# Gated DeltaNet in a two-layer trunk: decay, A and attention matrices built transposed, right-hand side and solution scaled differently

## The chip, the cores and the metric

The kernel runs on one core of one Trainium2 chip. The metric is the time of one execution in device microseconds (us), as the median of several runs. The engines are called PE (matrix products), DVE (vector), ACT (scalar, activations), POOL (GpSimd) and SP (which here only issues DMAs).

## The reference

The kernel computes a two-layer decoder trunk on 256 tokens of 1024 features, all in float32. Layer 0 mixes tokens by retention, layer 1 by gated DeltaNet; a SwiGLU channel mixer follows each. Only DeltaNet is touched. Its core, for 16 value heads of 128 features (two value heads share one of 8 key heads), is

```
gcum = cumsum(g)                                   # g: log decay of a token
decay[i, j] = exp(gcum[i] - gcum[j])   for i >= j, else 0
A    = beta * (k k^T) * decay          for i > j,  else 0
[u, w] = (I + A)^-1 [beta v, beta k exp(gcum)]
attn = (q k^T) * decay                 for i >= j, else 0
v_new = u - w S;   o = q exp(gcum) S + attn v_new
S = S exp(g_last) + (k exp(g_last - gcum))^T v_new
```

k and q are L2-normalised; a short causal convolution and a SiLU come before. The output is normalised per head, gated by silu(z) and projected. The reference uses chunks of 64 tokens; the kernel uses two chunks of 128, which is the same function.

## The kernel before

**Main stream.** The trunk is one list of jobs. A job has one slab of weights (512 KB): SP loads it (L130), ACT rounds it to a high part `whi` (L131), DVE forms the rest `wlo` (L133), and PE forms three products of it with the split activations (L139 to L141). Three buffers of each kind exist, so a slab cannot be loaded before an older one has been used. DeltaNet's jobs come in the order z0, k, q, z1, v0, z2, v1, v2, v3, z3, and then the output projection. For the k, q and v jobs, the convolution's taps are one ACT and three DVE instructions for each 128 channels (`taps`, L721 and L724).

**Tasks.** All that is particular to DeltaNet runs in generators that are advanced one step after each job. A planner then puts the instructions of each engine in an order, from program order and its own estimates; on the chip each engine works its list in that order, and waits on semaphores.

**The tasks the change touches**, in order of time:
- `gates`: log decays, beta, and the matrix `D` of decays of each chunk and head, as exp of a product with a triangular mask (`decay`, L714 and L715). `D` has the row token i on the partitions.
- `amat`, after each pair of key heads: `A` = k k^T scaled by `beta2` and `D` (L768 to L778); small scale vectors at L754 to L762.
- `invert`: the matrix `V` = ((I + A)^-1)^T. The 32 x 32 diagonal blocks of all heads and chunks are brought through DRAM to one block per partition (`Ab`, L797, L799). 31 steps of forward substitution follow on DVE, two instructions each: an outer product `pr` (L813) and a subtraction from `Vb` (L815). Step i works on n = i + 1 by m = 31 - i elements. `Vb` goes through DRAM once more (`Vd`, `Vc`, L820, L823), is copied into `Vf` and transposed into `Tc` (L832, L833); then the blocks are merged to 64 and 128 by products (L848 to L882).
- `attn`: q k^T (L913), copied by ACT (L915), multiplied by `D` on POOL into `att` (L916), and then in `flush` transposed by PE (four L200 for one instruction of POOL) and copied back by ACT into the place of `D` (L904). There are eight such rounds.
- `v_T`: transposes v and scales it, one ACT instruction for each head and chunk (L1098).
- `inner`, for each group of four heads: `solve` (products with `V`, L937, and a copy `uu` by ACT, L939), `du` (L959), products with keys, queries and the state (L951), `attend` (L945), the combination (L976), norm and gate.

The substitution is spread over the jobs by an estimate of its cost:

```
            V.tensor_tensor(tmp, Vb[:, 0:n, i:i + 1].broadcast_to([P, n, m]),
                            Ab[:, n:32, i].unsqueeze(1).broadcast_to([P, n, m]), ALU.mult)
            V.tensor_tensor(Vb[:, 0:n, n:32], Vb[:, 0:n, n:32], tmp, ALU.subtract)
            cost += 0.4 + 2 * n * m / 960
            if cost > b["pace"]:
```

Of the kernel before, what the change touches and what calls it, by code (L numbers as in the profile page):

```python
# [10 lines left out]
F32 = mybir.dt.float32  # L11
# [6 lines left out]
P = 128  # L18
D = 1024
# [11 lines left out]
def shape_constants():  # L31
    """Constants that depend on the shapes alone: identity, triangular masks,
    retention decay (with the key scale) and the rotary frequencies."""
# [14 lines left out]
def turn_pieces():  # L48
    """1 / (2 pi) cut into 12-bit pieces."""
# [12 lines left out]
class Trunk:  # L62
    """The main stream is a list of jobs, one weight slab each; tasks (generators)
    are advanced one step after every job, so that their small products and
    elementwise work lie between the large products."""
# [13 lines left out]
    # ------------------------------------------------------------ jobs and tasks  # L79
# [27 lines left out]
    def prefetch(self, ahead):  # L107
        """Loads slabs in the order of the jobs until ahead of them wait behind the next."""
        while self.todo and len(self.slabs) <= ahead:
            n = self.todo.pop(0)  # L110
            self.slabs[n] = self.slab(*self.jobs[n][1])

    # ---------------------------------------------------------------- helpers
# [9 lines left out]
    def slab(self, w, k0, nk, c0, ncol):  # L123
        """Rows [k0*128, (k0+nk)*128), columns [c0, c0+ncol) of w as the exact
        pair hi + lo of 12-bit parts."""
# [17 lines left out]
    def proj_tok(self, w, c0, ncol, xT, nk, done, parts=None, pair=(), tile_done=None):  # L143
        """[tokens, columns] products: one PSUM tile for each token tile, given to done.
        parts: ranges of the rows, other jobs may come between them (a list of lists of
        jobs is returned then). pair: numbers of slabs whose work on the second token
        tile waits for the next slab."""
# [3 lines left out]
        for n, k0 in enumerate(ks):  # L151

            def fn(hi, lo, n=n, k0=k0):
# [4 lines left out]
                for t, work in ((0, first), (1, held)):  # L158
# [3 lines left out]
                    # the second token tile not before the first where that one is wanted early  # L162
# [18 lines left out]
    def proj_chan(self, w, c0, xT, done):  # L181
        """[columns, tokens] products for 256 columns: one PSUM tile [128, 2, 256].
        A job is one block of 128 columns."""
# [18 lines left out]
    # ------------------------------------------------------------------ setup  # L202
# [63 lines left out]
    def load_gain(self, row):  # L266
        """A gain on all partitions."""
# [3 lines left out]
    # ------------------------------------------------------------------- norm  # L271
# [3 lines left out]
    def sumsq(self, half):  # L275
        """Adds up h^2 / D over a half of the features, for each token."""
# [5 lines left out]
    def rstd(self):  # L282
        """r[token tile] = (mean h^2 + eps)^-1/2 as [128, NT]."""
# [11 lines left out]
    def load_T(self, src, gain, half):  # L295
        """Half of the features of two [128, 1024] token tiles -> transposed, times
        the gain of each feature, as hi/lo pair in xh, xl [128, 8, 256]."""
# [15 lines left out]
    def rstd1(self, t):  # L313
        """(mean h^2 + eps)^-1/2 of one token tile, eps being in its first sum."""
# [12 lines left out]
    def out_proj(self, w, yT, nk, nxt, early=None):  # L327
        """h += y w, and what the next sublayer (kind, layer) needs of h. early: slabs of
        the first half done before those of the second half begin."""
# [56 lines left out]
    # -------------------------------------------------------------------- FFN  # L386
# [48 lines left out]
    # -------------------------------------------------------------- retention  # L435
    def rope_tables(self, b):
        """cos and sin of the rotary angles times r of the token: [128, 256]."""
# [159 lines left out]
    # ------------------------------------------------------------------ gated DeltaNet  # L597
# [12 lines left out]
    def normed(self, out, t, half, r):  # L610
        """Half of the features of h r gain, for one token tile."""
# [6 lines left out]
    def gdn_tokens(self, t, r):  # L618
        """Normalised, transposed tokens."""
# [13 lines left out]
    def gates(self, b):  # L633
# [52 lines left out]
        for c in range(NT):  # L686
            for hg in range(4):
# [5 lines left out]
                if len(pend) == 3:  # L693
                    self.decay(b, Ur, *pend.pop(0))
# [499 lines left out]
```

## Time and profile before

| | us |
|---|---|
| median of 3 runs | 874.71 |
| the three runs | 877.99, 874.71, 874.05 |
| span of the profiled execution, first to last instruction | 876.3 |

The profiled execution has no time of its own beside its span. DeltaNet's own work lies between about 420 and 660 us of the span. A profile gives for each engine how long it was busy, and for idle time the instruction that ended it; matmuls are pipelined, so that PE counts as busy from the start of one to the modelled end of the last.

### The profile page before, as it was taken

To read this page: it belongs to the slowest core of one execution; us is meant where nothing else is said; L and a number is where in the kernel's file an instruction comes from. 1 tells how busy PE (TensorE), PEld (TensorE's weight loads), DVE (VectorE), ACT (ScalarE), POOL (GpSimd) and SP (SyncE) were. 2 spreads that over 40 slices of the span, in tenths; PEclk is the share of its full clock that TensorE was granted. 3 is DMA by queue.
4 is the path that set the end of the run, shared out by engine and by line. 5 is a ranking of instruction groups with operands and counts; after the bars stand their busy time and mean duration, and the time that the engine had idled before them with its cause. 6 is when DMAs were issued, how large, how long until landed. Compare 5 with 4: busy or idle time off the path is not lost.

```text
span 876.3 us, 12736 instructions
## 1 busy us (share of the span) xinstructions
PE 845.1 (96%) x4903; PEld 722.0 (82%) x4903; DVE 555.6 (63%) x828; ACT 452.1 (52%) x770; POOL 58.8 (7%) x59
## 2 busy tenths in 40 slices
PE   6999999999999999999999988999899999999996
PEld 5889978887888888887998868998788888889885
DVE  4957877655555555545989899744665655555453
ACT  5543235654444444435587745667844544444343
POOL 1000000000000000000226240000200000000000
PEclk9999999999999999999999999899999999999999
DMA  8665455556666665563555744722046666665552
GB/s 247 210 196 168 123 158 153 190 171 215 171 190 187 179 189 175 185 192 107 158 145 122 211 122 131 208 76 74 1 147 189 193 187 179 188 191 171 190 192 72
DMA packets 121806, 143.54 MB, mean 164 GB/s; under 512 B 14145, under 2 KB 67826, under 8 KB 121746
## 3 DMA queue, kind: packets, MB, share of 16 engines
q1 hardware_dynamic: 121234, 141.48, 53.7%
q0 software_dynamic: 368, 1.19, 0.5%
q8 instruction: 38, 0.62, 0.3%
q14 instruction: 22, 0.18, 0.1%
q10 hardware_dynamic: 144, 0.07, 0.0%
HBM read 140.62 MB, written 2.10 MB: 163 GB/s over the span
## 4 chain that ended last, share of the span: by engine, by line
PE 37%; DVE 9%; DMA 2%; ACT 2%; issue 2%; POOL 1%; SPq 0%; POOLq 0%; ACTq 0%
PE mm L141 10%; PE mm L140 10%; PE mm L139 10%; DVE wlo L133 3%; DVE pr L813 2%; DVE cacc L724 2%; PE ip L951 1%; PE tp L200 1%; DVE Vb L815 1%; DMA raw<-gdn_w_in 1%; PE ip L937 1%; DMA Vd<-Vb 1%; PE ip L945 1%; DMA Vc<-Vd 1%; PE ip L856 0%
## 5 line engine op out<-in xcount | busy, mean ns | idle before, releaser
L133 DVE TENSOR_TENSOR wlo<-raw,whi 128x1024 fp32r<-128x1024 f32 x260 | 319.8, 1231 | 232.5 <-ACT whi L131 230.5
L131 ACT CAST whi<-raw 128x1024 fp32r<-128x1024 f32 x260 | 273.3, 1052 | 301.7 <-PE mm L140 227.5
L139 PE MATMUL mm<-whi,xh 128*128 128x512 f32 (+1 forms) x576 | 220.0, 385 | 2.0 <-ACT whi L131 1.3
L140 PE MATMUL mm<-whi,xl 128*128 128x512 f32 (+1 forms) x576 | 219.4, 381 | 0.5 <-DVE xl L311 0.3
L141 PE MATMUL mm<-wlo,xh 128*128 128x512 f32 (+1 forms) x576 | 207.6, 381 | 1.2 <-DVE wlo L133 1.2
L139 PEld LDWEIGHTS mm<-whi,xh 128*128 128x128 f32 x576 | 108.7, 189 | 21.9 <-ACT whi L131 1.8
L141 PEld LDWEIGHTS mm<-wlo,xh 128*128 128x128 f32 x576 | 108.2, 188 | 22.0 <-DVE wlo L133 2.1
L140 PEld LDWEIGHTS mm<-whi,xl 128*128 128x128 f32 x576 | 108.7, 189 | 20.7 <-issue 0.7
L139 PE MATMUL mm<-xh,whi 128*128 128x256 f32 x384 | 112.3, 293 | 0.0
L140 PE MATMUL mm<-xh,wlo 128*128 128x256 f32 x384 | 110.6, 288 | 1.2 <-DVE wlo L133 1.2
L141 PE MATMUL mm<-xl,whi 128*128 128x256 f32 x384 | 110.2, 287 | 0.0
L140 PEld LDWEIGHTS mm<-xh,wlo 128*128 128x128 f32 x384 | 74.7, 195 | 3.2 <-DVE wlo L133 1.8
L139 PEld LDWEIGHTS mm<-xh,whi 128*128 128x128 f32 x384 | 74.5, 194 | 1.4 <-issue 0.5
L141 PEld LDWEIGHTS mm<-xl,whi 128*128 128x128 f32 x384 | 74.5, 194 | 0.3
L139 PE MATMUL mm<-whi,hh 128*128 128x512 f32 x176 | 69.8, 397 | 0.0
L140 PE MATMUL mm<-whi,hl 128*128 128x512 f32 x176 | 69.6, 396 | 0.0
L141 PE MATMUL mm<-wlo,hh 128*128 128x512 f32 x176 | 64.3, 396 | 0.0
L724 DVE SCALAR_TENSOR_TENSOR cacc<-mm,conv,cacc 128x253 f32<-128x253 f32 (+2 forms) x96 | 45.6, 510 | 12.4 <-ACT cacc L721 11.8
L139 PE MATMUL mm<-whi,yh 128*128 128x512 f32 x128 | 49.5, 394 | 1.1 <-ACT yh L310 1.1
L140 PE MATMUL mm<-whi,yl 128*128 128x512 f32 x128 | 50.4, 394 | 0.0
L141 PE MATMUL mm<-wlo,yh 128*128 128x512 f32 x128 | 49.1, 396 | 0.0
L141 PEld LDWEIGHTS mm<-wlo,hh 128*128 128x128 f32 x176 | 33.1, 188 | 8.1
(235 smaller groups left out, 883.3 us busy)
## 6 DMA issues: line engine op xcount, KB each, us to landing
raw<-ffn_w_in SPq DMA_DIRECT2D x88, 512.0 KB, 3.6
raw<-ret_w_in SPq DMA_DIRECT2D x48, 512.0 KB, 4.1
raw<-gdn_w_in SPq DMA_DIRECT2D x48, 512.0 KB, 4.0
raw<-ffn_w_out SPq DMA_DIRECT2D x44, 512.0 KB, 3.6
raw<-ret_w_out SPq DMA_DIRECT2D x16, 512.0 KB, 3.3
raw<-gdn_w_out SPq DMA_DIRECT2D x16, 512.0 KB, 3.6
h<-x SPq DMA_DIRECT2D x4, 256.0 KB, 7.7
out<-o SPq DMA_DIRECT2D x4, 256.0 KB, 2.2
```

The source lines that it names most:

```text
L131: nc.scalar.copy(hi, raw)
L133: lo_ = nc.vector.tensor_tensor(lo, raw, hi.bitcast(F32), ALU.subtract)
L139: t.matmul(out, lh, rh, start=first, stop=False)
L140: t.matmul(out, ll, rh, start=False, stop=False)
L141: self.last_mm = t.matmul(out, lh, rl, start=False, stop=last).ins
L200: self.nc.tensor.transpose(out, in_, self.ident[:n, :n])
L724: self.nc.vector.scalar_tensor_tensor(acc[:, s:S], ps[:, 0:S - s], cw[:, i, blk:blk + 1], acc[:, s:S], ALU.mult, ALU.add)
L813: V.tensor_tensor(tmp, Vb[:, 0:n, i:i + 1].broadcast_to([P, n, m]), Ab[:, n:32, i].unsqueeze(1).broadcast_to([P, n, m]), ALU.mult)
L815: V.tensor_tensor(Vb[:, 0:n, n:32], Vb[:, 0:n, n:32], tmp, ALU.subtract)
L937: T.matmul(up[:, j], b["V"][c][:, 4 * hg + j], v[c][:, j], start=True, stop=True)
L945: T.matmul(op[:, j], b["D"][c][:, 4 * hg + j], uu[:, j], start=True, stop=True)
L951: T.matmul(f4(op[:, 2 * j:2 * j + 2]), x(2 * hg + j), f4(st[:, 2 * j:2 * j + 2]), start=True, stop=True)
```

## The change

- `D`, `A` and the attention matrix are built with the column token j on the partitions. For `D` the two triangular masks of the product swap places; the mask by POOL (L806) swaps its signs.
- The products q k^T become k q^T. Multiplied by the transposed `D` they have the orientation that `attend` wants. POOL writes into the place of `D`; the 32 transposes and 8 copies of `flush` and the buffer `att` are gone.
- The substitution reads row i of the transposed block (`Ab[:, i, n:32]`) where it read a column (`Ab[:, n:32, i]`).
- The merging products take the transposed `A`. The first of them (L848) reads `Tc` where it read `Vc`, the next ones `X` and `Vc` where they read `Tc` and `X`; their shapes stay.
- v is scaled by `kn`, the norm of its key (one ACT instruction for two heads instead of one for each), and the solution `uu` by `beta2` afterwards. That scaling is by DVE, from PSUM, where ACT copied. `beg` becomes `nege`, made once in `gates`; of the small instructions of `amat` three stay three.

Comments and docstrings left out:

```diff
         V.tensor_tensor(gl, g, gh.bitcast(F32), ALU.subtract)
-        Ur = self.t1("Ur", (P,), F32R)
-        V.tensor_copy(Ur, self.U)
+        Lr = self.t1("Lr", (P,), F32R)
+        V.tensor_copy(Lr, self.SL)
...
         b["beta"] = beta
-        slb = self.SL.unsqueeze(1).broadcast_to([P, 4, P])
+        b["nege"] = sm("nege", (NH,))
+        ub = self.U.unsqueeze(1).broadcast_to([P, 4, P])
...
                 for eng, x, y in zip((V, V if hg % 2 else G), gm, (gh.bitcast(F32), gl)):
-                    eng.tensor_tensor(x, slb, y[:, c, hs].unsqueeze(2).broadcast_to([P, 4, P]), ALU.mult)
+                    eng.tensor_tensor(x, ub, y[:, c, hs].unsqueeze(2).broadcast_to([P, 4, P]), ALU.mult)
...
                 if len(pend) == 3:
-                    self.decay(b, Ur, *pend.pop(0))
+                    self.decay(b, Lr, *pend.pop(0))
...
                     b["eg"], b["dec"] = eg, dec
+                    V.tensor_scalar(b["nege"], eg[:, 1], -1.0, None, ALU.mult)
         for x in pend:
-            self.decay(b, Ur, *x)
+            self.decay(b, Lr, *x)
...
-    def decay(self, b, Ur, c, hs, gm):
+    def decay(self, b, Lr, c, hs, gm):
...
         for i, x in enumerate(gm):
-            self.nc.tensor.matmul(dp, Ur, x.rearrange("p h j -> p (h j)"), start=i == 0, stop=i == 1)
+            self.nc.tensor.matmul(dp, Lr, x.rearrange("p h j -> p (h j)"), start=i == 0, stop=i == 1)
...
     def amat(self, b, sl):
...
         ks, hs = slice(2 * sl, 2 * sl + 2), slice(4 * sl, 4 * sl + 4)
+        k2 = self.ph.tile([P, NT, 2], F32, name="k2", bufs=2)
         rk = self.ph.tile([P, NT, 2], F32, name="rk", bufs=2)
-        V.tensor_scalar(rk, b["kss"][:, :, ks], EPS, None, ALU.add)
-        G.tensor_tensor(rk, rk, self.mhalf[:, 0:4].rearrange("p (t h) -> p t h", t=NT), ALU.pow)
-        yield
-        rkb = rk.unsqueeze(3).broadcast_to([P, NT, 2, 2])
+        V.tensor_scalar(k2, b["kss"][:, :, ks], EPS, None, ALU.add)
+        G.tensor_tensor(rk, k2, self.mhalf[:, 0:4].rearrange("p (t h) -> p t h", t=NT), ALU.pow)
+        yield
+        beta2 = b["beta2"]
+        V.tensor_tensor(b["kn"][:, :, ks], k2, rk, ALU.mult)
+        V.tensor_tensor(rk, rk, rk, ALU.mult)
         w2 = lambda x: x[:, :, hs].rearrange("p t (h w) -> p t h w", w=2)
-        beta1, beta2 = b["beta1"], b["beta2"]
-        V.tensor_tensor(w2(beta1), w2(b["beta"]), rkb, ALU.mult)
-        V.tensor_tensor(w2(beta2), w2(beta1), rkb, ALU.mult)
-        V.scalar_tensor_tensor(b["beg"][:, hs], beta2[:, 1, hs], -1.0, b["eg"][:, 1, hs], ALU.mult, ALU.mult)
+        V.tensor_tensor(w2(beta2), w2(b["beta"]), rk.unsqueeze(3).broadcast_to([P, NT, 2, 2]), ALU.mult)
...
                 dm = b["D"][c][:, hg * 4:hg * 4 + 4]
-                G.affine_select(dm, dm, [[0, 4], [-1, P]], ALU.is_ge, 0.0, base=0, channel_multiplier=1)
+                G.affine_select(dm, dm, [[0, 4], [1, P]], ALU.is_ge, 0.0, base=0, channel_multiplier=-1)
...
             V.tensor_tensor(tmp, Vb[:, 0:n, i:i + 1].broadcast_to([P, n, m]),
-                            Ab[:, n:32, i].unsqueeze(1).broadcast_to([P, n, m]), ALU.mult)
+                            Ab[:, i, n:32].unsqueeze(1).broadcast_to([P, n, m]), ALU.mult)
...
                 for h in range(NH):
-                    T.matmul(xp[b0, h], Am[c][b1, h, b0], Vc[b1, c * NH + h], start=True, stop=True,
-                             tile_position=(32 * q + 32, 32 * q))
-                A_.copy(X[b0], xp[b0])
+                    T.matmul(xp[b1, h], Am[c][b0, h, b1], Tc[b0, c * NH + h], start=True, stop=True,
+                             tile_position=(32 * q, 32 * q + 32))
+                A_.copy(X[b1], xp[b1])
...
                 for h in range(NH):
-                    T.matmul(vp[b0, h], Tc[b0, c * NH + h], X[b0, h], start=True, stop=True,
-                             tile_position=(32 * q, 32 * q))
+                    T.matmul(vp[b0, h], X[b1, h], Vc[b1, c * NH + h], start=True, stop=True,
+                             tile_position=(32 * q + 32, 32 * q))
...
                     for h in range(NH):
-                        T.matmul(tq[b1, h], X[b0, h], Tc[b0, c * NH + h], start=True, stop=True,
-                                 tile_position=(0, 32))
+                        T.matmul(tq[b1, h], Vc[b1, c * NH + h], X[b1, h], start=True, stop=True,
+                                 tile_position=(32, 32))
...
                     h = hg * 8 + j
-                    T.matmul(xp[lo, j], Am[c][up, h, lo], Vf[c][up, h, up], start=True, stop=True,
-                             tile_position=(64, 0))
-                X2.append(self.t2("X2", (8, 64), p=64))
-                A_.copy(X2[hg], xp[lo])
+                    T.matmul(xp[up, j], Am[c][lo, h, up], T2[lo, h], start=True, stop=True,
+                             tile_position=(0, 64))
+                X2.append(self.t2("X2", (8, 64))[up])
+                A_.copy(X2[hg], xp[up])
...
                     h = hg * 8 + j
-                    T.matmul(vp[lo, j], T2[lo, h], X2[hg][:, j], start=True, stop=True, tile_position=(0, 0))
+                    T.matmul(vp[lo, j], X2[hg][:, j], Vf[c][up, h, up], start=True, stop=True, tile_position=(64, 0))
...
-        def flush(c, hp, at):
-            tp = self.pstp().rearrange("p (x j) -> p x j", j=P)
-            for j in range(4):
-                self.transpose(tp[:, j], at[:, j])
-            nc.scalar.copy(b["D"][c][:, 4 * hp:4 * hp + 4], tp)
-
-        pend = None
...
             for hp in range(4):
-                at = self.t2("att")
...
                 for j in range(2):
-                    T.matmul(pp[:, j], b["qT"][:, 2 * hp + j, cs], b["kT"][:, 2 * hp + j, cs], start=True, stop=True)
+                    T.matmul(pp[:, j], b["kT"][:, 2 * hp + j, cs], b["qT"][:, 2 * hp + j, cs], start=True, stop=True)
...
                 nc.scalar.copy(kq, pp[:, 0:2])
-                G.tensor_tensor(at.rearrange("p (j w) x -> p j w x", w=2),
-                                b["D"][c][:, 4 * hp:4 * hp + 4].rearrange("p (j w) x -> p j w x", w=2),
-                                kq.unsqueeze(2).broadcast_to([P, 2, 2, P]), ALU.mult)
-                if pend:
-                    flush(*pend)
-                pend = (c, hp, at)
+                dv = b["D"][c][:, 4 * hp:4 * hp + 4].rearrange("p (j w) x -> p j w x", w=2)
+                G.tensor_tensor(dv, dv, kq.unsqueeze(2).broadcast_to([P, 2, 2, P]), ALU.mult)
                 yield
-        flush(*pend)
...
             uu = self.t2("uu")
-            A_.copy(f4(uu), f4(up))
+            V.tensor_tensor(uu, up, b["beta2"][:, c, hs].unsqueeze(2).broadcast_to([P, 4, P]), ALU.mult)
...
         for j in range(4):
-            V.scalar_tensor_tensor(v[1][:, j], kp[:, j], b["beg"][:, 4 * hg + j:4 * hg + j + 1], v[1][:, j],
+            V.scalar_tensor_tensor(v[1][:, j], kp[:, j], b["nege"][:, 4 * hg + j:4 * hg + j + 1], v[1][:, j],
...
             b["zs"] = [self.g4(f"zs{hg}", (NT, 4, P)) for hg in range(4)]
-            for n in ("beta1", "beta2"):
-                b[n] = self.ph.tile([P, NT, 16], F32, name=n)
-            b["beg"] = self.ph.tile([P, 16], F32, name="beg")
+            b["beta2"] = self.ph.tile([P, NT, 16], F32, name="beta2")
+            b["kn"] = self.ph.tile([P, NT, 8], F32, name="kn")
...
             for t in range(NT):
-                for j in range(2):
-                    h = 4 * hg + 2 * sl + j
-                    A_.activation(v[t][:, 2 * sl + j], tp[:, j, t], AF.Copy, scale=b["beta1"][:, t, h:h + 1])
+                h = 2 * hg + sl
+                A_.activation(v[t][:, 2 * sl:2 * sl + 2], tp[:, :, t], AF.Copy, scale=b["kn"][:, t, h:h + 1])
```

## Rows read from the trace of the kernel before

**Rows 1.** The page's first lines: busy us, share of the span, instructions.
```profile
span 876.3 us, 12736 instructions
PE 845.1 (96%) x4903; PEld 722.0 (82%) x4903; DVE 555.6 (63%) x828; ACT 452.1 (52%) x770; POOL 58.8 (7%) x59
```

**Rows 2.** Busy time of each engine in stretches of DeltaNet, with granted clock.
```profile
core 0: us, PE busy (x) PEld busy (x) DVE busy (x) ACT busy (x) POOL busy (x), PEclk, DMA share, GB/s
491.35:537.60 46.25, 39.55 (x278) 35.49 (x278) 45.46 (x76) 27.57 (x62) 15.43 (x9) 1.00 0.44 122
537.60:556.00 18.40, 17.91 (x145) 17.51 (x145) 15.39 (x32) 8.45 (x14) 0.00 (x0) 1.00 0.78 201
556.00:572.00 16.00, 15.32 (x228) 14.97 (x229) 11.26 (x20) 10.82 (x20) 0.00 (x0) 0.79 0.53 166
600.00:620.00 20.00, 20.00 (x147) 19.06 (x146) 7.13 (x18) 16.88 (x54) 0.00 (x0) 1.00 0.09 27
620.00:632.00 12.00, 8.84 (x46) 7.55 (x45) 8.80 (x31) 10.67 (x46) 3.27 (x2) 0.86 0.00 1
```

**Rows 3.** The chain that ended last: start us, us, what.
```profile
491.35 1.23 DVE wlo L133
...
536.33 1.22 DVE wlo L133
```

**Rows 4.** What PE waited for, 488 to 550 us: total us, times, longest.
```profile
PE tp L200 <- POOL att L916: 2.7, 3, 1.7
...
PE mm L140 <- DVE wlo L133: 1.2, 1, 1.2
```

**Rows 5.** Groups of instructions, 491 to 537.6 us: busy us, mean ns | idle before.
```profile
L813 DVE TENSOR_TENSOR pr<-Vb,Ab 128x156 f32<-128x156 f32 (+13 forms) x24 | 17.9, 745 | 0.3
...
L916 POOL TENSOR_TENSOR att<-D,kq 128x512 f32<-128x512 f32 x8 | 12.3, 1545 | 30.6 <-ACT kq L915 30.5
...
L200 PE MATMUL tp<-cst,att 128*128 128x128 f32 x32 | 5.0, 278 | 2.7 <-POOL att L916 2.7
L904 ACT COPY D<-tp 128x512 f32<-128x512 f32 x8 | 4.8, 605 | 0.0
```

**Rows 6.** DVE in order of time: start us, us, instruction (two steps of substitution).
```profile
498.33 0.45 DVE L813 TENSOR_TENSOR pr<-Vb,Ab 128x156 f32<-128x156 f32 x1
498.82 0.32 DVE L815 TENSOR_TENSOR Vb<-Vb,pr 128x156 f32<-128x156 f32 x1
...
518.59 0.63 DVE L813 TENSOR_TENSOR pr<-Vb,Ab 128x256 f32<-128x256 f32 x1
...
520.66 0.42 DVE L815 TENSOR_TENSOR Vb<-Vb,pr 128x256 f32<-128x256 f32 x1
```

**Rows 7.** One line by shape: ns min/median/max, first and last start us.
```profile
L691 DVE TENSOR_TENSOR gmh<-cst,gh x8: 677/680/1142, 424.7 to 437.9; 128x512 fp32r<-128x512 f32 x8
```

**Rows 8.** DVE and PE in order of time, 556 to 561 us [idle before <-releaser].
```profile
556.57 3.44 DVE L832 COPY Vf<-Vc 32x512 f32<-32x512 f32 x8 [2.45 <-DMA Vc<-Vd]
560.02 1.25 DVE L833 STREAM_TRANSPOSE Tc<-Vc 128x1024 f32<-128x1024 f32 x1
...
556.68 2.08 PE L848 MATMUL ip<-Vc,A 32*32 32x32 f32 x64 [1.14 <-DMA Vc<-Vd]
558.69 0.41 PE L141 MATMUL mm<-xl,whi 128*128 128x256 f32 x1
```

**Rows 9.** ACT, DVE and PE in order of time, 620 to 623 us.
```profile
621.12 0.56 ACT L939 COPY uu<-ip 128x512 f32<-128x512 f32 x1
...
621.72 0.69 DVE L959 TENSOR_TENSOR du<-uu,dec 128x512 f32<-128x512 f32 x1 [0.96 <-ACT uu L939]
...
622.56 1.10 PE L951 MATMUL ip<-du,kn 128*128 128x256 f32 x4 [2.06 <-DVE du L959]
```

**Rows 10.** Groups of instructions, the whole span: busy us, mean ns | idle before.
```profile
L1098 ACT ACTIVATE v<-tp,beta 128x128 f32<-128x128 f32 x32 | 9.1, 375 | 0.5 <-PE tp L200 0.5
L939 ACT COPY uu<-ip 128x512 f32<-128x512 f32 x8 | 4.7, 586 | 1.0 <-PE ip L937 1.0
```

## The prediction

> **What bounds the kernel now.** I read the page's first lines first. PE counts as busy for 96% of a span of 876.3 us [rows 1], so on average the kernel is bound by its products; but the change lies in one part of the span, so the table of busy time by stretch decides. There the reader should look at the first row of [rows 2]. From 491.35 to 537.60 us, DVE is busy for 45.46 of 46.25 us while PE is idle for 6.70. Against that, DVE has 63% over the whole span [rows 1]. So one stretch of 46 us is bound by DVE, and it is the stretch in which the 31 steps of substitution run beside the slabs' `wlo` and the taps.
>
> Then I read the chain that ended last, to see whether DVE's fullness there costs time. It goes from `wlo` to `wlo` on DVE from 491.35 to 536.33 us [rows 3], and PE's waits have the matching entry: 1.2 us once, for a `wlo` [rows 4]. That wait ends when this `wlo` ends, at about 537.5 us. At that point PE had used up all that it could do, and what comes later starts from DVE's time. PE's other waits in the stretch, 2.7 us for POOL's `att` [rows 4], lie before that point: taking them away alone lets PE reach the same `wlo` sooner and wait there longer.
>
> After 537.6 us PE is the bound again (17.91 of 18.40 us busy) [rows 2]. [...]
>
> **The removed transposes, copies and waits.** 32 transposes were at most 5.0 us of PE, the eight copies 4.8 us of ACT, and with them goes the 2.7 us that PE waited for `att` [rows 5]. All lie between 491 and 537.6 us. ACT is busy for 27.57 of the 46.25 us there, so its 4.8 us are hidden by DVE. PE would need 39.55 - 5.0 = 34.6 us there, and DVE, with the saving below, 45.46 - 3.9 = 41.6 us. DVE is still the longer, so I take 0 for PE's part. Its other bound is the whole, 5.0 + 2.7 = 7.7 us, if DVE's list is ordered so that PE no longer waits for it. POOL's eight products stay (12.3 us [rows 5]); they write into `D` instead of `att`, same size, same number.
>
> **The substitution's read.** L813 and L815 work on the same number of elements, and L815 reads and writes runs of m adjacent elements while L813 reads `Ab` 32 elements apart. At 156 elements they take 0.45 and 0.32 us, at 256 elements 0.63 and 0.42 [rows 6]: 0.13 / 156 = 0.83 and 0.21 / 256 = 0.82 ns for each element more. L813 also reads one element of `Vb` again and again for each row, which the change keeps, so the excess could come from that. [Rows 7] speak against it: L691 repeats one element along 128 others, both sources in SBUF, and takes 680 ns for 512 elements. L815's slope is (0.42 - 0.32) / 100 = 1.0 ns for each element, which from 0.32 us at 156 gives 0.32 + 0.356 = 0.68 us at 512. So a repeated element costs nothing, and the stride carries the excess. 24 of the 31 steps' L813 start in the stretch [rows 5]; without the one that starts behind the last `wlo`, these are the steps with n = 3 to 25, and n x (32 - n) adds up to 4784 elements: 4784 x 0.82 = 3.9 us. This lies on the chain to 537.5 us, and I take it in full: -3.9 us. The bounds are 0, if the repeated element costs after all in this shape, and -3.9. The steps left (581 elements) give 0.5 us more to the end of `Vb`.
>
> L813 took 17.9 us in the stretch [rows 5]; by the two rates it would be 24 x 0.16 + 4940 x 1.82 ns = 12.8 us. The other 5 us are single long instructions. POOL's products run in the same stretch and stay, so I let these 5 us stay.
>
> [...]
>
> **The merge.** L848 now reads `Tc`. In the profile `Vc` is there at 556.57 us, DVE makes eight copies into `Vf` (3.44 us) and then `Tc` (1.25 us), so `Tc` is there at 561.27, 4.70 us later [rows 8]. What PE puts in between decides. If its list has the slab products first that now follow L848 at 558.69 us [rows 8], nothing is lost; if L848 keeps its place, PE waits up to 4.70 us more, and behind it stand all slab products, as PE works in order. In the other direction, the wait of 1.14 us may go, and with it the low clock: 16 us at 0.79 [rows 2] lose 16 x 0.21 = 3.4 us, an estimate. So the bounds are -4.5 and +4.7 us, or +8.1 with another such stretch of low clock. I take 0: the planner knows the new dependence, and `Vb` is there 0.5 us earlier in relation to PE.
>
> **The solution's scaling.** `uu` moves from ACT (0.586 us, eight times [rows 10]) to DVE. The nearest DVE row is `du` [rows 9], 512 elements with a repeated factor: 0.69 us. That is 8 x 0.69 = 5.5 us more on DVE and 4.7 less on ACT. From 600 to 620 us DVE is busy for 7.13 of 20 us and PE for all [rows 2], so six of the eight are covered; without cover all eight would cost 8 x 0.11 = 0.9 us. At 620 us it helps: the products were done at 622.56 - 2.06 = 620.50, ACT began `uu` at 621.12 and DVE had been idle since 621.72 - 0.96 = 620.76 [rows 9]. DVE would do `uu` to 621.45 and `du` to 622.14, where `du` ended at 622.41: -0.3 us. The bounds are +0.9 and -2.06, the whole wait.
>
> **Edits at no cost.** v's scaling, 32 instructions of ACT to 16 larger ones, is at most 9.1 us of ACT [rows 10] where ACT is not the bound; if it were, half of it, 4.5 us, would be gained. The triangular masks, POOL's mask and the small vectors of `amat` keep number and shape; `nege` is one small instruction more, in a part where PE leads.
>
> **The sum.** -3.9 + 0 + 0 - 0.3 = -4.2 us. The profiled execution has only its span, 876.3 us, 1.6 above the median of the runs; the difference is taken from the median: 874.7 - 4.2 = 870.5 us. Faster or slower here means by over 0.5% (4.4 us), about what a measurement of this kernel can tell from no change; so the forecast lies on the edge of it.
>
> **The rivals.**
> - *Forecast, 870.5 us (868 to 872.5), chance 0.45.* DVE's stretch shortens by the cheaper read, PE's savings stay hidden.
> - *PE's savings pay, 866.7 us, chance 0.22.* DVE's list is planned anew and lets `wlo` go ahead of substitution steps; then PE gains its 7.7 us, with the 0.3: 874.7 - 8.0. With the cheaper read on top it would be 862.8. For it speaks that PE is busy for 96% elsewhere; against it that DVE has 0.8 us idle in 46.
> - *The stride is not the cost, 874.4 us, chance 0.18.* L813 keeps its times, PE's savings turn into longer waits for `wlo`, and only the 0.3 is left. Against it stand [rows 6, 7].
> - *L848 waits for `Tc`, up to 878.6 us, chance 0.15.* L848 keeps its place in PE's list, waits 4.70 us more, and another stretch of low clock costs 3.4: 870.5 + 8.1. From 4.2 us of added cost on, the kernel is slower than before. For it speaks that PE waits there already [rows 8], so that its list trusts too early an arrival; against it that slab products, which need no `Tc`, follow it in the list and can go first [rows 8].
>
> **Numbers.** Faster by over 0.5%: 0.22 + half of the forecast's 0.45, less a little, 0.43. Slower by over 0.5% needs nearly the whole of the last case: 0.10. Within: 0.47. The range leaves out the far ends of the second and the last case: 864 to 877.5 us.
>
> **What would show it.** In the new profile L813 at 256 elements should take about 0.42 us as L815 does (the third case if it stays at 0.63). The DVE-bound stretch should be about 4 us shorter, PE idle in it for more than 6.7 us, and a wait of PE for a `wlo` at its end; if PE waits less in it, the second case holds. At the merge, PE's wait before L848 and the clock after it tell the last case. `uu` should take 0.69 us on DVE and PE's wait for `du` shrink a little. I am wrong if the order on DVE changes much, or if the clock around the merge turns out otherwise than before.

## The result and the profile after

The changed kernel takes 883.55 us, median of 18 runs (880.75 to 885.91). The kernel before, run beside it, takes 877.21 us, median of 18 (873.07 to 882.66). The ratio is 1.007, 95% interval 1.0055 to 1.0084: slower by 0.7%, where 0.5% less was forecast (870.5 us, range 864 to 877.5). The profiled execution has a span of 880.4 us and a time of 882.13 us of its own. Of the 13.05 us between the forecast and the result, 2.5 are the base: the prediction started from 874.71 us, the median of three runs.

The busy time by stretch answers to [rows 2]:

```profile
core 0: us, PE busy (x) PEld busy (x) DVE busy (x) ACT busy (x) POOL busy (x), PEclk, DMA share, GB/s
491.35:537.60 46.25, 40.43 (x287) 36.79 (x287) 45.27 (x84) 24.63 (x51) 15.21 (x9) 1.00 0.51 144
537.60:556.00 18.40, 18.40 (x156) 18.40 (x155) 16.46 (x37) 10.43 (x17) 0.00 (x0) 1.00 0.78 212
556.00:572.00 16.00, 9.91 (x124) 8.87 (x123) 8.82 (x16) 3.70 (x6) 0.00 (x0) 0.83 0.51 135
572.00:588.00 16.00, 16.00 (x208) 15.09 (x206) 4.33 (x9) 10.22 (x21) 0.00 (x0) 0.50 0.00 1
```

The DVE-bound stretch is as full as before (45.27 of 46.25 us), and 84 instead of 76 DVE instructions fit into it. PE is idle in it for 46.25 - 40.43 = 5.82 us, less than the 6.70 before; by the prediction's own signs that points to its second case, in which PE's savings pay. The loss comes later: PE has 6.1 us idle between 556 and 572 us, and from 572 to 588 us it is busy throughout at a granted clock of 0.50.

What PE waited for from 480 to 680 us (total us, times, longest) answers to [rows 4, 8, 9]:

```profile
PE ip L851 <- DVE Tc L836: 6.1, 1, 6.1
PE mm L141 <- DVE wlo L133: 2.5, 2, 1.5
PE mm L140 <- DVE wlo L133: 2.1, 1, 2.1
PE ip L941 <- DVE du L949: 1.7, 1, 1.7
```

The waits for `att` are gone and those for `wlo` have grown from 1.2 to 4.6 us, which was forecast as the sign of savings of PE that stay hidden; the idle time of the whole stretch says otherwise, and experiment 2 decides between the two. L851 (L848 before) waits 6.1 us for `Tc`, where L848 waited 1.1 for `Vc`. DVE in order of time tells where `Tc` comes from:

```profile
549.13 0.20 DVE L816 TENSOR_TENSOR pr<-Vb,Ab 128x31 f32<-128x31 f32 x1
549.70 1.23 DVE L133 TENSOR_TENSOR wlo<-raw,whi 128x1024 fp32r<-128x1024 f32 x1 [0.38 <-ACT whi L131]
550.85 0.48 DVE L726 SCALAR_TENSOR_TENSOR cacc<-mm,conv,cacc 128x253 f32<-128x253 f32 x1
551.24 0.21 DVE L818 TENSOR_TENSOR Vb<-Vb,pr 128x31 f32<-128x31 f32 x1
...
562.58 3.44 DVE L835 COPY Vf<-Vc 32x512 f32<-32x512 f32 x8 [3.01 <-DMA Vc<-Vd]
566.03 1.25 DVE L836 STREAM_TRANSPOSE Tc<-Vc 128x1024 f32<-128x1024 f32 x1
```

Between the last two instructions of the substitution (L816, L818) stand a `wlo` and a tap of the convolution (L726), and DVE makes the eight copies ahead of `Tc`. The substitution ends at 551.45 us; before, it ended at 546.8, although its reads were dearer there. So the first merging product starts 10.7 us later than before: 4.7 us by the end of the substitution, 1.3 by a slower way through DRAM (11.1 against 9.8 us), 4.7 by the copies and `Tc`. DVE's groups from 480 to 560 us show both (first the changed kernel, then the kernel before; busy us, mean ns):

```profile
L133 DVE TENSOR_TENSOR wlo<-raw,whi 128x1024 fp32r<-128x1024 f32 x25 | 32.0, 1281 | 6.6 <-ACT whi L131 6.6
L726 DVE SCALAR_TENSOR_TENSOR cacc<-mm,conv,cacc 128x253 f32<-128x253 f32 (+2 forms) x40 | 19.0, 476 | 0.1
L816 DVE TENSOR_TENSOR pr<-Vb,Ab 128x31 f32<-128x31 f32 (+15 forms) x31 | 13.5, 436 | 1.1 <-DMA Ab<-Ad 0.8
```

```profile
L133 DVE TENSOR_TENSOR wlo<-raw,whi 128x1024 fp32r<-128x1024 f32 x21 | 25.9, 1231 | 4.2 <-ACT whi L131 4.2
L813 DVE TENSOR_TENSOR pr<-Vb,Ab 128x31 f32<-128x31 f32 (+15 forms) x31 | 19.8, 638 | 0.3
L724 DVE SCALAR_TENSOR_TENSOR cacc<-mm,conv,cacc 128x255 f32<-128x255 f32 (+2 forms) x35 | 16.7, 478 | 0.1
```

The 31 reads fell from 19.8 to 13.5 us, more than the 4.4 forecast (3.9 in the stretch, 0.5 behind). The stride is 4.2 of these 6.3 us: with the strided read in the changed kernel, and all else in the same order, the reads take 17.7 (experiment 3). The other 2.1 us are among the "single long instructions" that the prediction let stay. Before, five of the 31 reads took 1.3 to 1.7 us, each of them while POOL worked on a product of its own; in the changed kernel three do. One of the five, with the read that follows it, and POOL's products (two merged into one line) beside it:

```profile
505.73 1.63 DVE L813 TENSOR_TENSOR pr<-Vb,Ab 128x231 f32<-128x231 f32 x1
...
508.89 0.60 DVE L813 TENSOR_TENSOR pr<-Vb,Ab 128x240 f32<-128x240 f32 x1
```

```profile
505.32 3.21 POOL L916 TENSOR_TENSOR att<-D,kq 128x512 f32<-128x512 f32 x2
```

From 480 to 560 us DVE has four more `wlo` and five more taps than before. The cheaper read did not make this room: with the dear read the order on every engine is the same (experiment 3). It is the order planned for the new work: the slabs' work was drawn forward, and the substitution did not end sooner.

PE in order of time around the merge:

```profile
560.94 0.39 PE L141 MATMUL mm<-wlo,xh 128*128 128x512 f32 x1
567.42 3.24 PE L851 MATMUL ip<-Tc,A 32*32 32x32 f32 x61 [6.09 <-DVE Tc L836]
...
584.27 3.43 PE L851 MATMUL ip<-Tc,A 32*32 32x32 f32 x64
587.63 0.80 PE L139 MATMUL mm<-whi,xh 128*128 128x512 f32 x1
```

From 560.94 to 587.63 us PE begins no slab product, since those that stood there in its list before have been done ahead. Before, a slab product stood directly behind the first 64 merging products [rows 8], and 64 of them took 2.08 us; here the second 64 take 3.43. PE's groups over the merge (first changed, then before):

```profile
L851 PE MATMUL ip<-Tc,A 32*32 32x32 f32 x128 | 6.8, 236 | 6.1 <-DVE Tc L836 6.1
L875 PE MATMUL ip<-T,A 64*64 64x64 f32 x64 | 5.7, 267 | 0.0
L139 PE MATMUL mm<-whi,xh 128*128 128x512 f32 x10 | 4.7, 466 | 0.0
```

```profile
L141 PE MATMUL mm<-xl,whi 128*128 128x256 f32 x24 | 8.1, 336 | 0.0
L139 PE MATMUL mm<-whi,xh 128*128 128x512 f32 x16 | 6.3, 396 | 0.0
```

With their sisters (three products for each part of a slab) these are 30 slab products of 512 columns inside the changed kernel's merge, against 48 of 512 and 70 of 256 before.

On the chain that ended last stand `Tc` and L851, so all of this sets the end: `inner` needs the merge, and the slab work that could stand beside it is used up.

```profile
566.03 1.26 DVE Tc L836
567.42 3.24 PE ip L851 x61
```

From the end of the last merging product to the last instruction lie 276.8 us, and 276.7 before: in the two profiles the whole difference arises ahead of that end.

### The profile page after: what moved, and what is told of

Read it like the earlier page. It is cut to its first block, busy times and chain, and to the rows that moved or that the text cites. A ratio compares the mean times of both kernels' runs of the same rounds, so it can differ in the third digit from the quotient of the medians.

```text
span 880.4 us, 12671 instructions
## 1 busy us (share of the span) xinstructions
PE 844.9 (96%) x4871; PEld 723.8 (82%) x4871; DVE 554.6 (63%) x837; ACT 442.6 (50%) x738; POOL 61.1 (7%) x59
## 4 chain that ended last, share of the span: by engine, by line
PE 40%; DVE 8%; DMA 2%; issue 1%; ACT 1%; POOL 1%; SPq 0%; POOLq 0%; DVEq 0%; ACTq 0%
PE mm L140 11%; PE mm L141 11%; PE mm L139 11%; DVE wlo L133 2%; DVE cacc L726 2%; PE tp L200 1%; PE ip L941 1%; DVE pr L816 1%; DMA Vd<-Vb 1%; PE ip L851 1%; PE ip L935 1%; PE ip L927 1%; DVE Vb L818 1%; DMA Ab<-Ad 1%; PE ip L875 1%
## 5 line engine op out<-in xcount | busy, mean ns | idle before, releaser
L140 PEld LDWEIGHTS mm<-whi,xl 128*128 128x128 f32 x576 | 109.2, 190 | 20.5 <-issue 0.7
L726 DVE SCALAR_TENSOR_TENSOR cacc<-mm,conv,cacc 128x253 f32<-128x253 f32 (+2 forms) x96 | 44.4, 476 | 21.4 <-ACT cacc L723 20.8
```

The source lines that it names most:

```text
L140: t.matmul(out, ll, rh, start=False, stop=False)
L726: self.nc.vector.scalar_tensor_tensor(acc[:, s:S], ps[:, 0:S - s], cw[:, i, blk:blk + 1], acc[:, s:S], ALU.mult, ALU.add)
```

## Experiments

Two theories stood first. **W**: the new dependence on `Tc` costs its wait. **O**: the new order leaves too few slab products for the merge, whatever the wait. After the first four runs O gave way to **C**: PE pauses, then issues only small merging products, and the granted clock falls; the clock, not the order as such, is the second cost.

All runs in one table. The places are read from each kernel's profiled execution, us from its start: the end of the last L818 (L815), the first merging product, the last one's end; then the slab products that PE begins in between and the granted clock there. "Before" is the kernel before; its medians beside the runs were 877.67 (experiments 1 to 4), 877.75 (5 to 8) and 877.24 us (9 to 12). Differences in the text are of medians. Between kernels of different groups the ratios are the safer measure; where they tell another number it stands beside.

| kernel | median us | ratio to before [95%] | substitution ends | merge | slab products in it | clock in it |
|---|---|---|---|---|---|---|
| before | | | 546.8 | 556.7 to 599.6 | 118 | 0.92 |
| changed | 883.55 | 1.007 [1.0055, 1.0084] | 551.4 | 567.4 to 603.5 | 30 | 0.68 |
| 1 `Vc` read | 877.82 | 1.0012 [0.9995, 1.0028] | 551.4 | 562.5 to 598.5 | 30 | 0.72 |
| 2 before, no flush | 871.46 | 0.9932 [0.991, 0.9954] | 553.0 | 563.7 to 594.7 | 48 | 1.00 |
| 3 strided read | 885.25 | 1.0094 [1.0069, 1.0119] | 554.0 | 569.5 to 605.9 | 30 | 0.68 |
| 4 pace 2 | 883.76 | 1.0069 [1.0045, 1.0093] | 547.1 | 561.2 to 596.0 | 78 | 0.90 |
| 5 products added | 877.21 | 0.9994 [0.9977, 1.0012] | 554.0 | 570.7 to 600.4 | 30 | 1.00 |
| 6 `Tc` first | 878.46 | 1.0006 [0.9988, 1.0025] | 551.9 | 564.2 to 599.5 | 30 | 0.71 |
| 7 `Tc` first, pace 1.6 | 873.24 | 0.9953 [0.9935, 0.9971] | 544.9 | 557.6 to 592.9 | 82 | 1.00 |
| 8 as 2, reads `Tc` | 877.23 | 0.9992 [0.9972, 1.0012] | 552.0 | 566.2 to 600.8 | 40 | 0.80 |
| 9 as 1, products added | 875.75 | 0.9987 [0.996, 1.0014] | 554.0 | 566.0 to 597.3 | 30 | 0.95 |
| 10 as 6, products added | 874.67 | 0.9991 [0.9957, 1.0025] | 551.0 | 565.1 to 594.8 | 30 | 1.00 |
| 11 as 7, strided read | 878.62 | 1.0005 [0.9987, 1.0022] | 549.1 | 561.6 to 601.4 | 82 | 0.87 |
| 12 as 7, `uu` on ACT | 874.15 | 0.9968 [0.995, 0.9987] | 546.1 | 557.7 to 594.5 | 82 | 0.95 |

**1. The merge reads `Vc`.** One operand of the merge's first products is then the untransposed block; sizes stay.

```
-  T.matmul(xp[b1, h], Am[c][b0, h, b1], Tc[b0, c * NH + h], ...
+  T.matmul(xp[b1, h], Am[c][b0, h, b1], Vc[b0, c * NH + h], ...
```

> The changed kernel, but the first merging product reads Vc where it read Tc, so that part of the inverse is computed from the wrong operand; the order of all instructions on every engine stays as in the changed kernel. Theory W (the wait for Tc): the product's wait of 6.1 us shrinks by the 4.7 us that DVE needs after Vc, and some of the low clock behind it goes too: 4.7 to 8 us less than the changed kernel, 875 to 879 us, level with the kernel before. Theory O (the order: too few slab products are left when the inverse is ready, so that the merge stands bare on PE): the wait shrinks, but the copies between the merging products still show, as does the low clock: at most 4.7 us less, 879 us or more.

883.55 to 877.82 us: when its first merging products need no `Tc`, the kernel gains 5.7 us (5.1 by the ratios). The wait and the windows from 560 to 600 us:

```profile
PE ip L851 <- DMA Vc<-Vd: 1.2, 1, 1.2
```

```profile
560.00:580.00 20.00, 17.94 (x262) 16.46 (x261) 8.45 (x17) 11.79 (x23) 0.00 (x0) 0.64 0.29 74
580.00:600.00 20.00, 20.00 (x252) 17.55 (x250) 9.24 (x13) 13.22 (x23) 0.00 (x0) 0.85 0.32 107
```

The wait for `Tc` is gone and the clock is still low, after a pause of only 1.2 us: at 0.50 from 565.5 to 586.0 us, where the changed kernel has it from 566.5 to 590.4. So a second cost was left, and a part of the 5.7 us is a shorter stretch of low clock.

**2. The kernel before without the flushes.** `attn` writes the product into `D` and leaves out the 32 transposes and the eight copies; the attention is then untransposed.

```
-  if pend:
-      flush(*pend)
-  pend = (c, hp, at)
+  dv = b["D"][c][:, 4 * hp:4 * hp + 4].rearrange("p (j w) x -> p j w x", w=2)
+  G.tensor_tensor(dv, dv, kq.unsqueeze(2)..., ALU.mult)
```

> The kernel before, without the 32 transposes and 8 copies of the attention; POOL writes its product into the place of the decay, and the attention so stays untransposed, which changes the output. Strided read, orientation of the merge and the copy of uu by ACT are those of before. Theory O: the planner moves the slab products that fill the gap ahead of the merge (8.4 us of them stand ahead of the first merging product in its list, more than before), so nothing is gained in spite of 7.7 us less for PE: 876 to 882 us. Theory W, in which the removed work is a gain or hidden and the loss is the wait for Tc alone: 869 to 877 us.

871.46 us, 6.2 under the kernel before. The substitution ends 6.2 us later than before and the merge begins 7.0 us later, yet it ends 4.9 us sooner: what seems to count is all of PE's work up to the merge's end, of which less is left, and the clock stays up. The clock's part can be bounded: in the two profiles it is at 0.50 for 13.6 us in all before and for 8.4 us here. Half of that difference, 2.6 of the 6.2 us, is the most that can be its own, an estimate.

```profile
560.00:580.00 20.00, 20.00 (x345) 18.23 (x344) 12.23 (x23) 14.04 (x28) 0.00 (x0) 1.00 0.39 116
580.00:600.00 20.00, 20.00 (x244) 17.89 (x241) 10.92 (x16) 16.03 (x32) 0.00 (x0) 1.00 0.33 107
```

O as it was put on record (876 to 882 us) fell here: with 48 slab products instead of 118 in its merge, this kernel is the fastest of all. That the 30 of the changed kernel are too few is not excluded by that.

**3. The strided read put back** into the changed kernel (the substitution then reads its matrix by the other index and solves another system).

```
-  Ab[:, i, n:32].unsqueeze(1).broadcast_to([P, n, m]), ALU.mult)
+  Ab[:, n:32, i].unsqueeze(1).broadcast_to([P, n, m]), ALU.mult)
```

> The changed kernel, but the substitution reads a column of Ab again, 32 elements apart (of the transposed block, so that the inverse is wrong); order as in the changed kernel. If the chain of the substitution sets the time, as both theories have it for the changed kernel, L816 at 256 elements goes from 0.41 to 0.63 us, the 31 steps become 4.5 us longer, and so does the kernel: 887 to 889 us. If DVE's time in this stretch is covered, 883 to 884 us.

885.25 us, 1.7 more (2.1 by the ratios), between the two expectations. The intervals of the two ratios overlap, so the times alone do not tell it from 0 or from 4.4 us. The profiles point to about 2: the merge begins 2.1 and ends 2.4 us later, at the same clock of 0.68.

**4. The substitution packed more densely** (`b["pace"] = 2` instead of 1: twice as much of it between two jobs), which leaves more slab work for the merge.

> The changed kernel with twice as much of the substitution between two jobs (pace 2 for 1). Theory O: the inverse is ready with 18 us of slab products still to come in place of 7, so that the wait for Tc and the copies of the merge are covered: 868 to 876 us. Theory W: the wait for Tc stays, as it is put in the same place behind the landing: 880 to 884 us.

883.76 us, no gain, though the merge holds 78 slab products and ends 7.5 us sooner. The gain is lost to other waits of PE, here for the accumulators of the convolution, which leave slab work for behind the merge: from its end to the last instruction are 285.0 us instead of 276.8.

```profile
PE mm L139 <- DVE cacc L726: 7.8, 3, 4.0
...
PE ip L851 <- DVE Tc L836: 1.4, 1, 1.4
```

**5. Products that nobody reads**, put into the changed kernel's wait and merge.

```
+  def warm(n):
+      wt = Vc[:, 0:4].rearrange("p a b -> p (a b)")
+      wr = Vc[:, 0:16].rearrange("p a b -> p (a b)")
+      for _ in range(n):
+          T.matmul(self.psip(), wt, wr, start=True, stop=True)
+  warm(6)          # ahead of L851
   ...
+  if c == 0:
+      warm(1)      # ahead of each of the three later groups
```

> The changed kernel with nine added products whose results nobody reads: six (128x128x512, fp32) on the values' block ahead of the merge's first product, where TensorE waited 6.1 us for the transposed block, and one ahead of each of the three later groups of chunk 0's merging products. They cost some 2.6 us beyond the wait that they fill. [...] Rival W alone (the wait itself is the cost and the clock a symptom that costs nothing further): the time of the changed kernel plus the added work, 884 to 887 us, ratio 1.007 to 1.011.

By C the added work wins time, by W alone it costs time. 877.21 us: 6.3 us (6.7 by the ratios) won by adding work. Each added product stands as two records in the profile, so nine are x18.

```profile
560.00:580.00 20.00, 18.56 (x229) 12.81 (x228) 7.44 (x14) 7.58 (x14) 0.00 (x0) 1.00 0.34 82
580.00:600.00 20.00, 20.00 (x297) 17.07 (x296) 10.32 (x16) 15.13 (x28) 0.00 (x0) 1.00 0.26 84
```

```profile
L845 PE MATMUL ip<-Vc 128*128 128x512 f32 x18 | 8.7, 608 | 1.4 <-DMA Vc<-Vd 1.4
```

The merge begins at 570.7 us, 3.3 later than in the changed kernel, with the same 30 slab products and three added ones in it, and takes 29.7 instead of 36.1 us. The nine added products take 8.7 us, so the three in the merge about 2.9; by this estimate the low clock costs some 6.4 + 2.9 = 9.3 us there. The clock is a cost of its own, not a mark of the wait.

**6. `Tc` made ahead of the eight copies.**

```
+  V.transpose(Tc..., Vc...)
   for c in range(NT):
       for q in range(4):
           ...
           V.tensor_copy(Vf[c][qs, :, qs], Vc[qs, c * NH:(c + 1) * NH, :])
-  V.transpose(Tc..., Vc...)
```

> The changed kernel with the transposed block made from the values' block directly ahead of the eight copies instead of behind them. It should be there 3.4 us sooner, the wait of 6.1 us falls to about 2.7. Theory W: 3.4 us gained of the 5.7 that reading the values' block instead gained, about 880 us, ratio 1.003. Theory C: the same if a shorter pause does not change the clock; the clock from 560 to 600 us stays between 0.65 and 0.85, since the merge still stands without slab products between. If the clock recovers, 875 to 877 us.

878.46 us, 5.1 less (5.6 by the ratios), about what experiment 1 won, by a wait of 2.5 instead of 6.1 us. The clock stays low (0.71): a shorter pause does not mend it.

**7. `Tc` first and a pace of 1.6.** The edit of 6, and `b["pace"] = 1.6`.

> As the run with the transposed block ahead of the copies, and the planner is told to spread the slab products by a pace of 1.6 instead of 1, so that by its own costs 15 us of slab work instead of 6.8 are left when the merge begins. Theory C: slab products stand between the merging products again, the clock from 560 to 600 us is above 0.9, no long pause at the transposed block, 868 to 874 us, ratio 0.989 to 0.996, so under the kernel before. Against it: the pace leaves TensorE waiting elsewhere, as pace 2 did for the accumulators (7.8 us); then 878 to 884 us.

873.24 us, ratio 0.9953 [0.9935, 0.9971]: 10.3 us under the changed kernel, and under the kernel before. The windows:

```profile
560.00:580.00 20.00, 20.00 (x339) 17.90 (x338) 6.43 (x8) 10.89 (x20) 0.00 (x0) 1.00 0.33 107
580.00:600.00 20.00, 18.96 (x186) 16.64 (x184) 12.71 (x20) 14.22 (x30) 0.00 (x0) 1.00 0.33 107
```

PE waits for no `Tc`, 82 slab products stand in the merge, and the clock is 1.00. The pace has its price here too, 2.9 us of waiting for an accumulator, less than in experiment 4.

**8. The kernel of experiment 2, its merge reading `Tc`** (so the attention is untransposed and one operand of the merge is the other block).

> The kernel before without the flushes (as in the run without them, attention left untransposed) and with the merge's first products reading the transposed block, which DVE makes behind the eight copies. By the planner's costs 9 us of slab work are left at the merge. Theory W: the wait for the transposed block comes up here too, 4 to 6 us, and the time is that of the run without flushes plus 4 to 6: 875 to 877.5 us, ratio 0.998 to 1.001. Theory C adds: if in that wait and merge the clock falls to 0.65 to 0.85, up to 880 us; if slab products fill in and the clock stays, 871 to 873 us, ratio 0.993 to 0.996, and then neither the dependence nor the missing flush alone is the cost but the two with the order planned around them.

877.23 us, 5.8 more than without the dependence (5.3 by the ratios). The wait itself is only 1.6 us, and the merge begins 2.5 us later:

```profile
PE ip L848 <- DVE Tc L833: 1.6, 1, 1.6
```

The clock in the merge is 0.80 instead of 1.00, and it takes 3.6 us longer with eight slab products fewer. So the dependence alone undoes what leaving out the flushes gave, by the profiles the larger part of it through the clock.

**9. Neither wait nor bare merge**: the edit of 1 (one operand changed) and four added products.

> The changed kernel with both costs of the merge taken away: its first products read the values' block (one operand of the merge is wrong then, same sizes), and four added products (128x128x512, fp32, results unread) stand in it: one ahead of the first merging product, one ahead of each of the three later groups of chunk 0. Theory C (wait and clock are two costs that add up): the run on the values' block alone (ratio 1.0012) still had the clock at 0.64 and 0.85 from 560 to 600 us, the run with added products alone (0.9994) still had the wait; both together give a clock of 1.00, and after the added work of 4 times 0.85 us a gain of 3 to 6 us on either of them, 871 to 875 us, ratio 0.993 to 0.998. If the two are one cost, paid once: 877 to 880 us, ratio 1.000 to 1.003.

875.75 us, between the two expectations and with an interval that overlaps both, so this run does not decide between them. Ten of its twelve runs lie between 873.2 and 877.8 us, two at 882.3 and 884.4 with a mean clock of 0.981. In the profiled run the clock is 1.00 from 560 to 580 us and 0.91 from 580 to 600.

**10. `Tc` first and six added products.**

> The changed kernel with the transposed block made ahead of the copies (wait 2.5 us instead of 6.1) and six added products: three in that wait, one ahead of each of the three later groups of chunk 0's merging products. It still computes what the reference asks for. Theory C: clock 1.00 from 560 to 600 us, and 3 to 6 us under the run with the earlier block alone (ratio 1.0006), 872 to 876 us, ratio 0.994 to 0.998. If the clock was a symptom only: 878 to 882 us, ratio 1.001 to 1.005.

874.67 us, 3.8 under experiment 6 and within the expected times by the median. The ratio of 0.9991 is above the expected 0.994 to 0.998, its interval holds 1, and by the ratios only 1.3 us are won on experiment 6. For the runs fall into two groups: eight lie between 872.8 and 875.0 us (mean clock 0.993 to 0.997), four between 883.0 and 886.1 (0.982 to 0.984). In its profiled run, one of the eight, the merge takes 29.7 us at a clock of 1.00, against 35.2 at 0.71 in experiment 6.

**11. Experiment 7 with the strided read** (again another system is solved).

> The run with the earlier transposed block and pace 1.6 (ratio 0.9953), with the substitution reading its matrix 32 elements apart again, as the kernel before does. It tells what the read is worth where the merge has neither the wait nor the low clock. The forecast's term: 3.9 us in the bound stretch and 0.5 behind it, 877 to 878 us, ratio 0.9995 to 1.001. If the read is worth as little as in the changed kernel itself (1.7 us): 874 to 876 us, ratio 0.996 to 0.998.

878.62 us, 5.4 more than experiment 7; by the ratios 0.5%, or 4.6 us, give or take 2.2. DVE's group, as above:

```profile
L816 DVE TENSOR_TENSOR pr<-Vb,Ab 128x31 f32<-128x31 f32 (+15 forms) x31 | 17.7, 571 | 1.2 <-DMA Ab<-Ad 0.8
```

The substitution ends 4.1 us later, close to the 17.7 - 13.5 = 4.2 us of reads. In the profiled run a clock of 0.87 in the merge adds some 4.6 us to that (39.8 against 35.3 us with the same 82 slab products), more than the medians show; the profiled run of 7 was its shortest. Here the forecast's 4.4 us are found, within that noise.

**12. Experiment 7 with `uu` copied by ACT**; the row factor is left out.

> The run with the earlier transposed block and pace 1.6 (ratio 0.9953), with uu copied by ScalarE in one instruction instead of multiplied by its factor on VectorE; the factor is left out. It tells what the move of uu is worth. The forecast's term of 0.3 us: 873 to 874.5 us, within 0.5 us of that run, ratio 0.995 to 0.997. If the move costs VectorE its cover where it waits (there VectorE's uu is waited for 0.9 us): 872 to 873 us, ratio 0.993 to 0.995. If ScalarE's queue is in the way: 875 to 877 us.

874.15 us, 0.9 more than experiment 7 (1.3 by the ratios), with intervals that overlap. The move of `uu` is worth little either way, as the forecast had it.

## Why the prediction was wrong

**The failed step is the merge, taken as 0.** The prediction had the dependence, its 4.70 us and the low clock behind it as the last rival (0.15) and as bounds, and set it to nothing because "slab products, which need no `Tc`, follow it in the list and can go first". They did go first, but earlier: the planned order had drawn them ahead, and when `Tc` was waited for none stood next in PE's list, for 26.7 us from the last one's start to the next one's. Leaving out the flushes did that (48 slab products in the merge of experiment 2, 118 before), and the dependence added to it (40 in experiment 8); the cheaper read had no part (30 with either read, in experiment 3 and in the changed kernel). So PE waited 6.1 us, and then the small products ran alone at a granted clock of 0.50. Experiments 1 and 8 put 5.7 and 5.8 us on the dependence, its effect on the clock included; experiment 6 won nearly as much by a shorter wait alone; experiment 5 puts some 9 us on the clock. The two overlap: with the wait gone or shorter and products added, 7.8 and 8.9 us were won by the medians (9, 10; 7.3 and 6.9 by the ratios), less than their sum. The rival's mechanism was right and its price too small: the wait grew by 4.95 us, near its 4.70, but it gave only 3.4 us to the clock, and its 8.1 us were added to a gain that had been counted in full.

**PE's savings, taken as hidden (0), were not hidden in the kernel before.** Experiment 2 has them without the rest of the change and gains 6.2 us, of which at most some 2.6 are the clock's; the other bound was 7.7. The waits for `wlo` grew, as forecast, but the inference from the DVE-bound stretch was false: DVE's chain could end 6.2 us later and the merge still ended sooner, since slab products keep PE busy beside it. In the changed kernel this gain is there as slab work done sooner, and is spent again at the merge.

**The read, -3.9 us, was right for the instruction and depends on the place for the kernel.** L816 at 256 elements takes 0.41 us, as forecast:

```profile
522.17 0.41 DVE L816 TENSOR_TENSOR pr<-Vb,Ab 128x256 f32<-128x256 f32 x1
...
524.03 0.41 DVE L818 TENSOR_TENSOR Vb<-Vb,pr 128x256 f32<-128x256 f32 x1
```

Before, it took 0.63 us [rows 6]: 0.22 / 256 = 0.86 ns for each element more. The source's elements lie 32 apart there, and side by side in the changed kernel. The stride was the cost (the 31 reads take 17.7 us with it and 13.5 without, experiment 3), so the third case ("the stride is not the cost") fell. In every second step the rows of `Ab` are read from an odd element on. No cost of that shows: the step behind the one of 256 elements is such a step, and takes 0.42 us:

```profile
524.48 0.42 DVE L816 TENSOR_TENSOR pr<-Vb,Ab 128x255 f32<-128x255 f32 x1
```

The gain for the kernel is some 2 us in the changed kernel (3 against the result, not clear of noise) and 4.6 to 5.4 where `Tc` is not waited for (11 against 7).

**`uu`, -0.3 us**: 0.69 us on DVE, as forecast, and a wait for `du` of 1.7 instead of 2.06 us. Experiment 12 can't tell it from nothing.

**In sum**: -4.2 us forecast, +6.3 measured. Two of the gains are there (6.2 us in experiment 2, without the rest of the change; 4.6 for the read in 11); that of `uu` is not shown. Where the order and the early `Tc` keep the merge covered, 873.24 us come out, 0.5% under the kernel before.

**What stays open**: how the pause and the missing wide products share in lowering the clock. In the five kernels with a clock of 0.80 or less in the merge PE paused for at least 1.2 us ahead of it and had fewer slab products in it than in experiments 2 and 7. The traces narrow it down. A pause alone is not enough: in experiments 5 and 10 PE pauses 1.4 and 1.5 us, wide added products follow, and the clock stays at 1.00. Nor is a pause needed: in experiments 11 and 12 PE is busy throughout the merge, and the clock still falls to 0.50, three times and once, for 3.4 us each.

```profile
560.00:580.00 20.00, 20.00 (x288) 18.30 (x287) 8.78 (x14) 8.91 (x14) 0.00 (x0) 0.91 0.34 107
580.00:600.00 20.00, 20.00 (x244) 16.55 (x244) 7.83 (x12) 12.82 (x24) 0.00 (x0) 0.83 0.28 92
```

(Both rows are of experiment 11.) With pauses of the same length and many slab products in the merge, in the kernel before (1.1 us, 118) and in experiment 4 (1.4 us, 78), the clock falls twice for 3.4 us; with 30, in experiment 1 (1.2 us), once for 20.5 us. So how long the low clock lasted went with how much slab work stood behind the pause. And experiment 9 does not settle whether wait and clock add up.

## What to carry to other kernels

Time freed on an engine can be spent on filler work, done sooner; look up at which dependent chain that filler is missing next, and price the chain bare, its clock included (here a wait of 6.1 us and, by the estimate of experiment 5, some 9 us of low clock). Where an edit adds a producer behind a transfer, put that producer first on its engine: one moved line gave back 5.1 of the 6.3 us here. And when a dependence is moved, plan the order anew with it: the same change with `Tc` first and a denser substitution is faster than both kernels.

## What the hardware showed unexpectedly

PE was busy for 16.00 of 16.00 us from 572 to 588 us, filled with products of 32 x 32 and 64 x 64 and eight transposes, and the granted clock was 0.50 throughout. In experiment 1 the clock was 0.64 from 560 to 580 us after a pause of 1.2 us. In experiment 5 nine products of no use, 8.7 us of work, brought the clock in the changed kernel's merge from 0.68 to 1.00 and made the kernel 6.3 us faster.

And executions of one and the same kernel differ along with it: in experiment 10, 872.8 to 875.0 us at a mean clock of 0.993 and more, 883.0 to 886.1 at 0.984 and less.

Some reads of the substitution took about 1 us longer than those of like size beside them (1.63 us for 231 elements against 0.60 for 240), each of them during a product of POOL. The convolution's taps in the same places kept their 0.47 us. Why is not shown.
